# Splitting two projections by columns and keeping weight blocks, so that the norms behind them can start early

## The chip, the cores and the metric

The kernel runs on the 8 cores of one Trainium2 chip, as one program launched once. Cores 0 and 1 take sequence 0 of the batch, cores 2 and 3 sequence 1, and so on; each core produces 1024 of the 2048 tokens of its sequence and reads all weights itself. The metric is device time in microseconds (us) of the slowest core. A program on eight cores has a second, slower state in some executions, in which the cores of one die get a lower TensorE clock; such runs are set aside, and only fast runs are compared.

Words used below: PE is TensorE, the matmul engine; PEld are its weight loads; DVE is VectorE, ACT ScalarE, POOL the engine whose queue issues the weight loads from HBM, SP another issuing queue. PSUM is the memory that matmuls write; the kernel uses it in banks of 512 fp32 columns.

## The reference, cut to what matters

```python
x += concat(y_c, y_m) @ W_out                          # output projection
x += W_down( silu(g) * u ),  [g, u] = dwconv3_causal(RMSNorm(x) @ W_up) + b
x += sigmoid(RMSNorm(x) @ W_pg) * (p[i] @ W_pp)        # gate stage
out = RMSNorm_final(x)

def rmsnorm(x, g):
    y = xf * lax.rsqrt(jnp.mean(xf * xf, axis=-1, keepdims=True) + EPS)
    return (y * g.astype(jnp.float32)).astype(x.dtype)
```

D_MODEL is 2048 (16 blocks of 128 features), D_FF is 5632 (44 blocks), D_PLE 256. The norm runs over features. The kernel keeps features on the 128 partitions and tokens along the columns, so the sum of squares over features needs all 16 blocks of the projection before it, and then a sum over partitions, which PE does as a matmul with a matrix of ones. That is why a norm between two projections tends to stop PE: the next projection's first matmul needs the scaled input, and the scaling needs the last output of the projection before.

## The kernel before

Weights come in blocks of 1024 KB (bf16 in SBUF), into four slots, in the order of tasks. A task is a block and what is done with it; `again` uses a block that is still in its slot.

```python
wo_at = [task(blk(w_out_b, b), 16, 256, wout_task(b, (0, 1), 0)) for b in range(8)]   # pass one: slices 0 and 1
call(norm2_begin)
for n, b in enumerate((4, 5, 6, 7)):                                                   # pass two: slice 2
    again(wo_at[b], wout_task(b, (2,), 8))
    if n == 0:
        call(lambda: [norm2_stat(0), norm2_stat(1)])
    call(lambda n=n: norm2_apply(n // 2, range(8 * (n % 2), 8 * (n % 2) + 8)))
for b in range(4):
    task(blk(w_out_b, b), 16, 256, wout_task(b, (2,), 8))                              # four blocks loaded again
```

So the output projection was already split: 1026 columns in three slices, two in pass one and the third in pass two, with the second norm's sum (`norm2_stat`) and scaling (`norm2_apply`) of the first two under pass two. The down projection and the third norm were not split. The feed-forward part runs in three groups of 16, 16 and 12 blocks of D_FF; each ends in eight down-projection tasks:

```python
def wdown_task(g0, gn, cb, last):
    def consume(slot, Rs):
        if last and cb == 0:
            table_preload()
        for j in range(2):
            f = 2 * cb + j
            ps, Rb = feat_major_proj(slot, Rs, j, aT, RaT[0:gn], gn, wd_slices, k_outer=(cb == 0 and j == 0))
            P.op("dve", ... xres[:, f, 5:1029] += ps ...)          # 1024 columns
            if last:
                sumsq_hook(f, 5, 1024, f == 0)                     # ACT square, DVE add into acc
...
def norm3():
    ...
    norm_finish_sliced(5, own_slices, C_G3, hT, RhT3, Rrs2_3)      # per half: sum on PE, rstd on ACT, 16 scalings on DVE
    P.op("pool", ... ppw <- w_pp ...); P.op("pool", ... pTb <- pT ...)
call(norm3)
```

The gate stage has 32 groups: for half s of the columns and feature block f, 16 matmuls of the gate, 2 of the projection of p, then sigmoid (ACT), product and add (DVE), square (ACT), add into the final norm's sum (DVE). Three pairs of PSUM banks go round. Between the halves stands the final norm's sum of half 0:

```python
for b in range(8):
    pg_task(b, 0)
call(lambda: final_rs(0))                                          # sum on PE, rstd on ACT
for b in range(8):
    pg_task(b, 1)
    call(lambda b=b: final_ops(0, [2 * b, 2 * b + 1]))             # final scaling and store of half 0
call(table_preload)
call(lambda: final_rs(1))
call(lambda: final_ops(1, range(16)))
```

Each engine runs its instructions in program order; waits are on semaphores, placed from what each operation reads and writes.

## Time and profile before

| | before |
|---|---|
| median of 5 runs, slowest core | 1776.13 us (1774.19 to 1777.12) |
| profiled execution | 1774.19 us; spans of the cores 1767.4 to 1772.6 us |
| mean granted TensorE clock of the cores | 0.983 to 0.986 |

How the views are read. A timeline line has the start, the length, the engine, the source line and operation, what it writes and reads, how many instructions are merged, and in brackets how long the engine was idle before it and what ended that idle time. The waits view has, per pair, the total, the count and the longest wait. The table by stretches has the stretch and, by engine, busy time and count, then the granted clock, the DMA share and GB/s. The prediction shows the lines on which it rests. One view that it names but does not show is the list of PE's waits from 540 us on:

```profile
PE psC L1085 <- DVE regE L1080: 7.1, 2, 3.6
...
PE psC L462 <- DVE regE L457: 4.0, 1, 4.0
...
PE psA L1063 <- DVE hT L466: 2.2, 6, 0.7
...
PE psB L869 <- DMA wsl<-w_out_b: 1.7, 1, 1.7
```

L1085 is the final norm's sum (twice, half 0 and half 1), L462 the third norm's sum, L1063 a gate matmul that waits for its scaled input, and L869 the output projection that waits for a reloaded block. These four are what the change works on (of L1085 only half 0's wait).

### The profile page before, as it was taken

To read this page: it belongs to the slowest core of one execution; us is meant where nothing else is said; L and a number is where in the kernel's file an instruction comes from. 1 tells how busy PE (TensorE), PEld (TensorE's weight loads), DVE (VectorE), ACT (ScalarE), POOL (GpSimd) and SP (SyncE) were. 2 spreads that over 40 slices of the span, in tenths; PEclk is the share of its full clock that TensorE was granted. 3 is DMA by queue.
4 is the path that set the end of the run, shared out by engine and by line. 5 is a ranking of instruction groups with operands and counts; after the bars stand their busy time and mean duration, and the time that the engine had idled before them with its cause. 6 is when DMAs were issued, how large, how long until landed. Compare 5 with 4: busy or idle time off the path is not lost.

```text
span 1772.6 us, 27638 instructions; the slowest of 8 cores (1767.4 to 1772.6 us)
## 1 busy us (share of the span) xinstructions
PE 1666.2 (94%) x11268; PEld 1070.4 (60%) x11310; DVE 737.0 (42%) x1092; ACT 389.5 (22%) x567; POOL 69.5 (4%) x134
## 2 busy tenths in 40 slices
PE   1999999989988998999999999999999999998995
PEld 1888868756655665666654466666445666443442
DVE  3543201233354474444431144444212544447556
ACT  3230032322332222222210022222001222222332
POOL 0000000000000000000000000000000000000000
PEclk9999999999999999999999999999999999998997
DMA  9944433433427657344433444333344333346774
GB/s 255 236 103 73 72 55 67 72 54 66 72 49 197 137 89 127 73 80 81 78 72 71 75 81 82 74 72 72 73 83 83 72 72 60 72 84 113 137 147 162
DMA packets 26156, 167.98 MB, mean 95 GB/s; under 512 B 3120, under 2 KB 3120, under 8 KB 8880
## 3 DMA queue, kind: packets, MB, share of 16 engines
q0 software_dynamic: 18976, 131.67, 41.6%
q1 hardware_dynamic: 7056, 34.55, 6.0%
q8 instruction: 91, 1.49, 0.3%
q14 instruction: 33, 0.27, 0.1%
HBM read 289.48 MB, written 8.39 MB: 168 GB/s over the span
## 4 chain that ended last, share of the span: by engine, by line
PE 89%; DVE 4%; DMA 2%; ACT 2%; issue 2%; DVEq 0%; SPq 0%; ACTq 0%; POOLq 0%
PE psB L518 34%; PE psA L518 26%; PE psB L504 9%; PE psA L1063 4%; PE psA L504 4%; PE psB L869 3%; PE psA L869 3%; PE psB L1063 2%; DMA arena<-xsl 2%; DMA wsl<-w_out_b 1%; DVE arena L1092 1%; PE psB L1067 0%; PE psC L413 0%; DVE hT L466 0%; ACT regE L662 0%
## 5 line engine op out<-in xcount | busy, mean ns | idle before, releaser
L518 PE MATMUL psB<-hT,wsl 128*128 128x344 bf16 (+2 forms) x3312 | 501.1, 312 | 8.7 <-DVE yT L739 8.7
L518 PEld LDWEIGHTS psB<-hT,wsl 128*128 128x128 bf16 x3312 | 324.4, 98 | 172.6 <-issue 9.5
L518 PE MATMUL psA<-hT,wsl 128*128 128x344 bf16 (+1 forms) x2160 | 326.8, 311 | 2.0 <-DVE regE L951 2.0
L518 PEld LDWEIGHTS psA<-hT,wsl 128*128 128x128 bf16 x2160 | 211.8, 98 | 109.9 <-issue 2.3
L518 PE MATMUL psA<-yT,wsl 128*128 128x512 bf16 x684 | 154.6, 378 | 2.1 <-DVE yT L988 1.0
L518 PE MATMUL psB<-yT,wsl 128*128 128x512 bf16 x694 | 155.3, 378 | 0.5
L947 ACT ACTIVATE regE<-psA,cst_sb 128x1026 f32<-128x1026 f32 x44 | 53.1, 1207 | 394.2 <-PE psA L518 385.7
L504 PE MATMUL psB<-wsl,hT 128*128 128x256 bf16 x1152 | 128.8, 274 | 0.0
L949 DVE SCALAR_TENSOR_TENSOR regE<-psA,cst_sb,regE 128x1026 f32<-128x1026 f32 x44 | 56.6, 1286 | 165.0 <-ACT regE L947 165.0
L504 PEld LDWEIGHTS psB<-wsl,hT 128*128 128x128 bf16 x1152 | 112.8, 98 | 13.6
L949 DVE SCALAR_TENSOR_TENSOR regE<-psB,cst_sb,regE 128x1026 f32<-128x1026 f32 x44 | 56.6, 1285 | 154.7 <-ACT regE L947 154.7
L518 PEld LDWEIGHTS psA<-yT,wsl 128*128 128x128 bf16 x704 | 68.1, 97 | 84.8 <-issue 1.5
L518 PEld LDWEIGHTS psB<-yT,wsl 128*128 128x128 bf16 x704 | 68.1, 97 | 83.9
L947 ACT ACTIVATE regE<-psB,cst_sb 128x1026 f32<-128x1026 f32 x44 | 53.0, 1205 | 166.8 <-PE psB L518 166.8
L1063 PE MATMUL psA<-hT,wsl 128*128 128x512 bf16 x344 | 85.6, 394 | 3.0 <-DVE hT L466 2.2
L975 ACT ACTIVATE regE<-regE 128x1026 f32<-128x1026 f32 x44 | 46.6, 1058 | 123.5 <-DVE regE L951 123.5
L1006 DVE TENSOR_TENSOR arena<-psB,arena 128x1024 f32<-128x1024 f32 x24 | 29.4, 1225 | 104.4 <-PE psB L518 104.4
L1006 DVE TENSOR_TENSOR arena<-psA,arena 128x1024 f32<-128x1024 f32 x24 | 29.4, 1225 | 93.2 <-PE psA L518 93.2
L1063 PEld LDWEIGHTS psA<-hT,wsl 128*128 128x128 bf16 x352 | 35.2, 100 | 52.0 <-issue 14.3
L869 PE MATMUL psB<-yT,wsl 128*128 128x342 bf16 (+2 forms) x384 | 57.5, 309 | 1.7 <-DMA wsl<-w_out_b 1.7
L951 DVE SCALAR_TENSOR_TENSOR regE<-psA,cst_sb,regE 128x1026 f32<-128x1026 f32 x44 | 56.6, 1286 | 4.6
L951 DVE SCALAR_TENSOR_TENSOR regE<-psB,cst_sb,regE 128x1026 f32<-128x1026 f32 x44 | 56.5, 1285 | 4.6
(161 smaller groups left out, 1371.6 us busy)
## 6 DMA issues: line engine op xcount, KB each, us to landing
wsl<-w_up_b POOLq DMA_DIRECT2D x44, 1024.0 KB, 8.8
wsl<-w_in_b POOLq DMA_DIRECT2D x30, 1024.0 KB, 10.2
wsl<-w_down_b POOLq DMA_DIRECT2D x16, 1024.0 KB, 8.7
wsl<-w_pg_b POOLq DMA_DIRECT2D x16, 1024.0 KB, 8.8
wsl<-w_out_b POOLq DMA_DIRECT2D x12, 1024.0 KB, 12.4
arena<-xr SPq DMA_DIRECT2D x4, 2058.0 KB, 24.5
arena<-xsl SPq DMA_DIRECT2D x8, 1024.0 KB, 11.2
arena<-xsl SPq DMA_DIRECT2D x4, 2048.0 KB, 16.1
```

The lines of the kernel that those rows point to most:

```text
L504: P.op("pe", lambda e, k=k, t=t, ps=ps: e.matmul(ps[:, 0:ncol], lhsT=src[:, k, t * 128:(t + 1) * 128], rhs=slot[:, k, 0:ncol], start=(k == ...
L518: P.op("pe", lambda e, k=k, si=si, c0=c0, w=w: e.matmul(ps[:, si, 0:w], lhsT=slot[:, k, j * 128:(j + 1) * 128], rhs=src[:, k, c0:c0 + w], ...
L869: P.op("pe", lambda e, k=k, ps=ps, c0=c0, w=w, j=j: e.matmul(ps[:, 0:w], lhsT=slot[:, k, j * 128:(j + 1) * 128], rhs=yT[:, k, c0:c0 + w], ...
L947: P.op("act", lambda e: e.activation(out=dst[:, :, :], in_=ps[:, :, 2:344], func=AF.Identity, bias=cs(C_FCB + cidx), scale=w2), reads=Rb + ...
L949: P.op("dve", lambda e: e.scalar_tensor_tensor(out=dst[:, :, :], in0=ps[:, :, 1:343], scalar=w1, in1=dst[:, :, :], op0=ALU.mult, op1=ALU.add),
L951: P.op("dve", lambda e: e.scalar_tensor_tensor(out=dst[:, :, :], in0=ps[:, :, 0:342], scalar=w0, in1=dst[:, :, :], op0=ALU.mult, op1=ALU.add),
L975: P.op("act", lambda e, j=j: e.activation(out=upg[j][:, :, :], in_=upg[j][:, :, :], func=AF.Silu), reads=[Rupg[j]], writes=[Rupg[j]])
L1006: P.op("dve", lambda e, ps=ps, f=f: e.tensor_tensor(out=xres[:, f, 5:1029].rearrange("p (s n) -> p s n", s=2), in0=ps[:, 0:2, 0:512], in1= ...
L1063: P.op("pe", lambda e, k=k, pg_=pg_, j=j: e.matmul(pg_[:, 0:512], lhsT=slot[:, k, j * 128:(j + 1) * 128], rhs=hT[:, k, 512 * s:512 * (s + ...
L1092: P.op("dve", lambda e, k=k, xs=xs: e.scalar_tensor_tensor(out=xs, in0=xs, scalar=cs(C_GF + k), in1=rs2[:, 512 * s:512 * (s + 1)], op0=ALU ...
```

## The change

Its intent: let every norm's sum and scaling of one part of the columns run under the projection of the other part, and avoid the waits for reloaded weight blocks. It has three parts.

1. Output projection: blocks 0 and 1 are loaded a second time, into free memory, while pass one runs; pass two takes them from there, in turn with the blocks still in slots, and reloads only blocks 2 and 3.
2. Last third of the down projection: two passes of 512 columns. Half 0's sum (`norm3_stat(0)`) and scaling run under pass two, half 1's sum comes after the first 16 gate matmuls, and its scaling goes in pairs into gate groups 1 to 8. Blocks 0 to 3 are loaded again (768 KB each). The loads of w_pp and p come earlier, into other memory.
3. The final sum of half 0 moves behind the gate matmuls of the second group of half 1.

```diff
-    wo_at = [task(blk(w_out_b, b), 16, 256, wout_task(b, (0, 1), 0)) for b in range(8)]
+    def load_wo_e():
+        for i in range(2):
+            P.alias(Rwo_e[i], conv_res + mlstm_small_res)
+            P.op("pool", lambda e, i=i: e.dma_start(out=wo_e[i], in_=blk(w_out_b, i)), writes=[Rwo_e[i]], dma=True)
+
+    wo_at = []
+    for b in range(8):
+        wo_at.append(task(blk(w_out_b, b), 16, 256, wout_task(b, (0, 1), 0)))
+        if b == 4:
+            call(load_wo_e)
     call(norm2_begin)
-    for n, b in enumerate((4, 5, 6, 7)):
-        again(wo_at[b], wout_task(b, (2,), 8))
+    second = [("again", 4), ("kept", 0), ("again", 5), ("kept", 1), ("again", 6), ("again", 7), ("load", 2), ("load", 3)]
+    for n, (how, b) in enumerate(second):
+        if how == "again":
+            again(wo_at[b], wout_task(b, (2,), 8))
+        elif how == "kept":
+            call(lambda b=b: wout_task(b, (2,), 8)(wo_e[b], Rwo_e[b]))
+        else:
+            task(blk(w_out_b, b), 16, 256, wout_task(b, (2,), 8))
 ... (cut: norm2_stat and norm2_apply as before; memory of ppw and pTb moved) ...
+    def last_down(cb, s, gn, first_f):
+        def consume(slot, Rs):
+            if s == 0 and cb == 0:
+                table_preload()
+            kcut = gn - 2 if (s == 0 and cb == 0) else gn
+            ... (cut: one PSUM bank for each of two row blocks) ...
+            if kcut < gn:
+                mm(0, range(kcut))
+                mm(1, range(kcut))
+            for j in range(2):
+                f = 2 * cb + j
+                ps, Rb = outs[j]
+                mm(j, range(kcut if kcut < gn else 0, gn))
+                xs = xres[:, f, 5 + 512 * s:5 + 512 * (s + 1)]
+                P.op("dve", ... xs += ps ...)
+                sumsq_late(f == first_f, xs, Rx2[f][s], acc[:, 512 * s:512 * (s + 1)], Racc2[s])
+        return consume
 ... (cut: sumsq_late, norm3_stat, norm3_apply, ple_loads, aliases) ...
+        for cb in range(8):
+            ld_at.append(task(blk(w_down_b, cb, 44)[:, g0:g0 + gn, :], gn, 256, last_down(cb, 0, gn, 0)))
+            if cb == 4:
+                call(ple_loads)
+        for n, cb in enumerate((4, 5, 6, 7)):
+            again(ld_at[cb], last_down(cb, 1, gn, 8))
+            if n == 0:
+                call(lambda: norm3_stat(0))
+            call(lambda n=n: norm3_apply(0, range(3 * n, 3 * n + 3)))
+        for cb in range(4):
+            task(blk(w_down_b, cb, 44)[:, g0:g0 + gn, :], gn, 256, last_down(cb, 1, gn, 8))
+            call(lambda cb=cb: norm3_apply(0, range(12 + 2 * cb, 14 + 2 * cb) if cb < 2 else ()))
 ... in pg_task, between the gate matmuls and the two matmuls of p ...
+                if s == 0 and f == 0:
+                    norm3_stat(1)
+                if s == 1 and f == 1:
+                    final_rs(0)
+                if s == 0 and 1 <= f <= 8:
+                    norm3_apply(1, range(2 * f - 2, 2 * f))
 ...
     for b in range(8):
         pg_task(b, 0)
-    call(lambda: final_rs(0))
     for b in range(8):
         pg_task(b, 1)
```

## The prediction

> **What bounds the kernel now.** I read the page first, then the busy time by stretches around the ends of the phases, then the timeline there, the landing times of single loads, and last the waits of PE.
>
> ```profile
> PE 1666.2 (94%) x11268; PEld 1070.4 (60%) x11310; DVE 737.0 (42%) x1092; ACT 389.5 (22%) x567; POOL 69.5 (4%) x134
> PEclk9999999999999999999999999999999999998997
> PE 89%; DVE 4%; DMA 2%; ACT 2%; issue 2%; DVEq 0%; SPq 0%; ACTq 0%; POOLq 0%
> ```
>
> These are the page's busy line, its clock line and its chain. PE is 94% busy and carries 89% of the chain, so time can only come off where PE stands still or runs slowly, and the change takes no matrix work away. The clock is at 9 (90% or more) everywhere but in two of the last slices. So I look for the places where PE waits within the changed stretch: the output projection (near 560 to 675 us) and everything from the last third of the down projection (1519 us) to the end.
>
> ```profile
> 1520.00:1600.00 80.00, 78.57 (x360) 35.16 (x366) 38.28 (x32) 17.17 (x18) 4.22 (x8) 1.00 0.47 85
> 1600.00:1610.00 10.00, 5.16 (x19) 1.72 (x18) 3.68 (x3) 2.62 (x4) 1.97 (x3) 0.90 0.46 85
> 1610.00:1625.00 15.00, 12.32 (x25) 3.28 (x27) 14.31 (x22) 3.69 (x5) 0.00 (x0) 0.61 0.84 141
> 1625.00:1690.00 65.00, 61.16 (x270) 27.23 (x274) 38.88 (x58) 20.69 (x34) 4.25 (x8) 0.97 0.72 130
> ```
>
> Columns: the stretch, its length, busy us and count of PE, PEld, DVE, ACT, POOL, then granted clock, DMA share, GB/s. Between 1600 and 1625 us PE does 44 matmuls in 25 us. The stretch before does 360 in 80. In 1610 to 1625 us DVE is the full one (14.31 of 15) and the clock falls to 0.61. This is the third norm. The timeline gives its edges:
>
> ```profile
> 1598.01 5.06 PEld L518 LDWEIGHTS psB<-yT,wsl 128*128 128x128 bf16 x24
> ...
> 1607.55 0.30 PEld L462 LDWEIGHTS psC<-regE,cst_sb 128*128 128x128 f32 x2 [4.48 <-issue]
> ...
> 1610.69 21.29 DVE L466 SCALAR_TENSOR_TENSOR hT<-arena,cst_sb,regE 128x512 bf16<-128x512 f32 x32 [3.26 <-ACT regE L393]
> ...
> 1622.76 4.78 PE L1063 MATMUL psA<-hT,wsl 128*128 128x512 bf16 x16
> ...
> 1627.16 0.31 PEld L1067 LDWEIGHTS psB<-yT 128*128 128x128 bf16 x2
> ```
>
> The last down-projection weight load ends at 1598.01 + 5.06 = 1603.07. The sum of squares (a matmul with ones) starts 4.48 us later, after the last add, square and add on DVE and ACT. The gate matmuls then follow the scaling of hT one k at a time, one per 0.665 us (21.29 / 32), until about 1622. The next group still runs slowly. Two groups of 18 matmuls are done at 1627.47.
>
> ```profile
> 1681.55 0.31 PEld L1067 LDWEIGHTS psA<-yT 128*128 128x128 bf16 x2
> ...
> 1685.90 0.30 PEld L1085 LDWEIGHTS psC<-regE,cst_sb 128*128 128x128 f32 x2 [4.04 <-issue]
> ...
> 1691.80 0.31 PEld L1067 LDWEIGHTS psB<-yT 128*128 128x128 bf16 x2
> ```
>
> This is the middle of the gate stage: the final norm's sum for half 0 stands between half 0 and half 1, waits 4.04 us, and the next group of 18 is done only at 1692.11.
>
> ```profile
> 669.23 4.49 PEld L869 LDWEIGHTS psB<-yT,wsl 128*128 128x128 bf16 x32 [2.07 <-issue]
> 669.26 4.81 PE L869 MATMUL psB<-yT,wsl 128*128 128x341 bf16 x32 [1.75 <-DMA wsl<-w_out_b]
> ...
> 675.24 2.18 PEld L968 LDWEIGHTS psA<-hT,wsl 128*128 128x128 bf16 x16 [1.52 <-issue]
> ```
>
> This is the second pass of the output projection. The last reloaded block is late, and then the first up-projection block. I asked for the landing of those two loads alone, issued at 653.83 and 658.48:
>
> ```profile
> wsl<-w_out_b POOLq DMA_DIRECT2D x1, 1024.0 KB, 15.2
> wsl<-w_up_b POOLq DMA_DIRECT2D x1, 1024.0 KB, 16.5
> ```
>
> They land at 669.0 and 675.0, which is when PE goes on. The wait at 675.24 is named by DVE in the waits, but the landing time says it is the load.
>
> **What the Trainium skill says.** "TensorE: Matmul & The Clock Gate", section "What's actually happening": after an idle window of some 3.4 us PE runs at half clock until it has been busy as long. The trace agrees: after the 4.48 us gap and the thin feeding the next gate matmuls come 0.43 us apart, against 3.34 / 15.5 = 0.216 us later, and also after the 4.04 us gap. "DMA: Bandwidth & Descriptors", section "Anatomy of one DMA — SWDGE (gpsimd) path": about 2.0 us fixed plus a part by size. Here a 1024 KB block takes 8.8 us alone (the page's median), while queued blocks land 6.4 to 6.5 us apart, so about 2.3 us is fixed; the skill's rate is not reached, and I use 6.5. "ScalarE: Activation LUTs", section "What ACT_TABLE_LOAD costs": about 1283 ns of load and as much again of drain. The trace has the load at 1.28 us; I see no such drain. "VectorE: DVE Perf Modes", section "The perf-mode tier table": a tensor_tensor on fp32 has only the plain mode. Here 1024 columns take 1.23 us and 512 take 0.69, so time follows width and about 0.15 us is paid per instruction; halves cost a little more DVE.
>
> **The change part by part.**
>
> Part one, the output projection. Its first pass begins at 558.5 and the second at about 633.2 (two thirds into 48 weight loads from 628.54). Eight tasks of 32 matmuls at 6.98 / 48 = 0.1454 us make 37.2 us, and the two sums of squares cost 1.06 us (637.82 to 638.88), so with no wait PE would reach the up projection at 671.5. It gets there at 675.24. The change keeps blocks 0 and 1 in a spare buffer, loaded in the first pass when DMA idles (its share in 600 to 640 us is 0.15), and reloads two blocks, not four. By the same pace blocks 2 and 3 are issued at 638.7 and 649.2 and wanted at 662 and 667; the first up block is issued at 658.5 into an empty queue, lands by 669.5 even with the 10.9 us that a load took here, and is wanted at 671.5. All waits go: 675.24 - 671.5 = 3.7 us. The later stall at 690 to 692 us, where both bank groups wait for their first evacuation, stays.
>
> Part two, the third norm. The last third of the down projection is done in two passes of 512 columns: the same 384 matmuls at 0.216 us, 83 us, plus four reloads of 768 KB (6.5 us to land, one per 5.2 us task, each wanted 15 us after issue: hidden). Sum, rstd and scaling of half 0 lie under pass two: per task of 5.18 us DVE has two evacuations (0.79 with its gap), two adds (0.70) and three scalings (0.665), 5.0 us, just enough. Half 1's sum comes after the first 16 gate matmuls (3.45 us), its last evacuation, square and add needing 0.6 + 0.69 + 0.15 + 0.6 + 0.1 + 0.69 + 0.12 = 2.95 us; no wait. A 512-column sum costs PE about 0.9 us (0.62 measured for 341 columns, by width). Two groups then end at 2 x 3.88 + 0.9 = 8.7 us after the down projection, against 1627.47 - 1603.07 = 24.4 now: 15.7 us saved. At the start of the last third PE waits for the last aT chunk as before; with 21 instead of 22 matmuls placed ahead it loses 0.2 us more.
>
> Part three, half 0's final sum moves behind the second group's gate matmuls of half 1. From 1681.86 to 1692.11 are 10.25 us; one group and the sum need 3.88 + 0.9 = 4.8: 5.5 us saved. The earlier loads of w_pp and p save nothing: they landed at 1614.5 and 1618.2, before PE's need at 1621.9.
>
> What is given back: DVE and ACT lag behind PE in the gate stage. One group's chain repeats every 3.07 us at best (product to product, 1652.46 to 1655.53). With two scalings it is 3.07 + 1.33 = 4.4 against PE's 3.88, so over groups 1 to 8 it falls back 8 x 0.5, on top of some 2.5 us from the switch of tables, to about 6 us behind. Three bank pairs allow the product some 11 us, so PE does not stop; groups 9 to 15 win it back at 0.8 each. The moved final sum, with two table loads, puts ACT and DVE some 3.8 us behind again at group 17. There the budget is thin: two groups with two final scalings need 7.38 of 7.76 us, so 7 pairs win back 0.38 x 7 = 2.7, and about 1 us is left when PE ends. It lengthens the tail (now 1750.4 to 1772.6) by 1.0.
>
> Sum: 3.7 - 0.2 + 15.7 + 5.5 - 1.0 = 23.7 us. 1776.1 - 23.7 = 1752.4.
>
> **The rivals.** First, a DVE bound: if scalings and evacuations cost more than I count, banks come free late and PE waits in pass two or in gate groups 5 to 9. For it: 5.0 of 5.18 and 4.4 against 3.88. Against it: the bank slack of 8 to 11 us. It would give back 2 to 8 us, to 1755 to 1760. Second, DMA: 3 MB of down blocks, 2 MB of output blocks and the earlier w_pp come on top on all eight cores; a late block costs what it is late. For it: queued blocks already land at 6.5 us each. Against it: each is wanted 9 us or more after its expected landing, except the first up block with 2 us. It would leave 1 to 3 us. Third, more gain: without the two waits before it, the stall at 690 us may not lower the clock; 48 matmuls there took 8.86 against 7.03 us, so 1.8 us more. Fourth, the gap moves: if PE met half 1's sum before it is ready, a wait of 1 us and no cold clock.
>
> **Range and chances.** The parts on PE are differences of measured times, certain to perhaps 3 us together; the lag at the end is 0 to 3 us; the rivals weigh more on the slow side. I say 1752, with 1747 to 1760. Faster by over 2% would need 35.5 us, while all the PE waits that I found in these stretches sum to 25: 0.02. Slower by over 2% would need a new bound: 0.01. Within 2%: 0.97.
>
> **What would show it.** Right: no DMA wait at the second pass; no PE gap over 2 us between the end of the down projection and the end of the gate stage; gate groups at 3.88 us from the first; clock near 1.00 there; two short sums on PE; PE's end to span's end 22 to 24 us. Wrong: waits of PE on DVE or ACT in the gate groups, a scaling still running when half 1 begins, a wait on a down block in pass two, or a tail over 25 us.

## The result, and the profile after

| | before | changed |
|---|---|---|
| median | 1776.35 us of 13 runs | 1754.78 us of 7 runs |
| range of the fast runs | 1774.01 to 1777.83 | 1754.27 to 1755.65 |
| ratio, changed over before | | 0.988, 95% interval 0.9869 to 0.989 |

Each has one run in the slow state (2061.2 and 1908.35 us), which is in the median and not in the range or the ratio. The ratio here and below is the mean time of one kernel's fast runs over that of the other's of the same rounds, so it is not quite the ratio of the medians. The kernel is 21.6 us faster by the medians, 1.2%, within the 2% that count as the same.

The page of the changed kernel (busy line, clock line, chain):

```profile
PE 1661.2 (95%) x11310; PEld 1071.5 (61%) x11310; DVE 737.6 (42%) x1123; ACT 391.0 (22%) x583; POOL 71.6 (4%) x138
PEclk9999999999999999999999999999999999999997
PE 89%; DVE 5%; ACT 2%; issue 2%; DMA 2%; DVEq 0%; ACTq 0%; SPq 0%
```

The 8 of the clock line is gone; the last digit, where PE has done its last work, is 7 before and after. The table by stretches, cut at the same events as in the prediction (last third of the down projection, first two gate groups, groups 16 and 17, tail):

```profile
1518.00:1603.00 85.00, 83.71 (x387) 37.40 (x386) 52.44 (x79) 23.37 (x36) 7.80 (x14) 1.00 0.74 126
1603.00:1612.00 9.00, 9.00 (x42) 4.05 (x40) 2.68 (x4) 3.74 (x5) 0.53 (x1) 1.00 1.02 164
...
1666.00:1675.00 9.00, 9.00 (x42) 4.04 (x41) 3.50 (x6) 2.68 (x5) 1.06 (x2) 1.00 0.71 130
...
1729.00:1752.00 23.00, 2.56 (x5) 0.52 (x3) 14.71 (x23) 4.46 (x7) 0.00 (x0) 0.59 0.61 210
```

The first two gate groups now take 9 us at a clock of 1.00 where they took 24.5, and PE is busy in all of it. In the last third DVE works 52 us of 85 where it worked 39.5 of 84 (lines of before in the prediction show 38.28 of 80). PE's waits from 1600 us to the end are down to one, the final sum of half 1:

```profile
PE psC L1172 <- DVE regE L1167: 4.2, 1, 4.2
```

The timeline of the second pass of the output projection (L869) into the up projection (L985, L518):

```profile
666.84 6.93 PEld L869 LDWEIGHTS psB<-yT,wsl 128*128 128x128 bf16 x48
...
673.82 2.30 PEld L985 LDWEIGHTS psA<-hT,wsl 128*128 128x128 bf16 x16
...
691.02 8.53 PEld L518 LDWEIGHTS psA<-hT,wsl 128*128 128x128 bf16 x48 [2.43 <-issue]
691.05 8.86 PE L518 MATMUL psA<-hT,wsl 128*128 128x344 bf16 x48 [2.10 <-DVE regE L968]
```

No line waits for a load any more: the up projection follows 0.05 us after the output projection's last weight load. The stall before 691.02 is still there, and the 48 matmuls after it take 8.86 us where the next 48 take 7.19. (The pause is 2.43 us in the weight loads and 2.10 in PE's matmuls, which lag behind them. The 2.24 us in some of the expectations is neither of the two.) The same block in the kernel before, on core 6 and on core 1:

```profile
692.21 8.86 PE L518 MATMUL psA<-hT,wsl 128*128 128x344 bf16 x48 [1.99 <-DVE regE L951]
```

```profile
693.98 7.19 PE L518 MATMUL psA<-hT,wsl 128*128 128x344 bf16 x48 [1.99 <-DVE regE L951]
```

The stall is equal on both; only on core 6 is the block behind it slow.

The timeline from pass one of the last third (L1046) into the gate stage (L1144 gate, L1154 the two matmuls of p, L1089 the sums of squares):

```profile
1565.99 0.40 PEld L1089 LDWEIGHTS psC<-regE,cst_sb 128*128 128x128 f32 x2
...
1597.92 5.06 PEld L1046 LDWEIGHTS psA<-yT,wsl 128*128 128x128 bf16 x24
...
1603.10 3.33 PEld L1144 LDWEIGHTS psA<-hT,wsl 128*128 128x128 bf16 x16
...
1606.56 0.41 PEld L1089 LDWEIGHTS psC<-regE,cst_sb 128*128 128x128 f32 x2
...
1611.30 0.31 PEld L1154 LDWEIGHTS psB<-regE,yT 128*128 128x128 bf16 x2
```

Half 0's sum stands inside pass two, half 1's after 16 gate matmuls, and two groups end at 1611.61, 8.63 us after 1602.98. And the tail (L1172 final sum, L1179 final scaling):

```profile
1728.71 0.31 PEld L1154 LDWEIGHTS psB<-regE,yT 128*128 128x128 bf16 x2
...
1733.68 0.50 PEld L1172 LDWEIGHTS psC<-regE,cst_sb 128*128 128x128 f32 x2 [4.66 <-issue]
1733.71 2.05 PE L1172 MATMUL psC<-regE,cst_sb 128*128 128x512 f32 x2 [4.19 <-DVE regE L1167]
...
1737.27 10.69 DVE L1179 SCALAR_TENSOR_TENSOR arena<-arena,cst_sb,regE 128x512 f32<-128x512 f32 x16 [2.39 <-ACT regE L393]
```

One core's profile is not enough here, since the slowest core was core 6 before and core 7 after. So I took the start or end of the weight loads that bound each phase on every core and made a table of phase lengths, the median of the eight cores (all in us). The spread over the cores is under 0.1 where none is given.

| phase | before | changed | difference | predicted |
|---|---|---|---|---|
| start to output projection | 558.3 (556.3 to 560.6) | 557.9 (554.7 to 560.7) | -0.4 | 0 |
| output projection, pass one | 74.70 | 74.70 | 0 | 0 |
| output projection, pass two | 41.75 (41.0 to 44.0) | 38.38 | -3.4 | -3.7 |
| up projection to last third of down | 842.28 (842.2 to 844.0) | 844.16 | +1.9 | 0 |
| last third of down projection | 83.93 | 85.00 | +1.1 | +0.2 |
| gate groups 0 and 1 | 24.3 (24.0 to 24.4) | 8.63 | -15.7 | -15.7 |
| gate groups 2 to 15 | 54.39 | 54.39 | 0 | 0 |
| gate groups 16 and 17 | 14.13 (14.0 to 14.1) | 8.63 | -5.5 | -5.5 |
| gate groups 18 to 31 | 54.39 | 54.39 | 0 | 0 |
| tail, from PE's last projection matmul | 22.3 (21.6 to 23.1) | 23.0 (22.5 to 23.7) | +0.7 | +1.0 |
| sum | | | -21.3 | -23.7 |

(Groups 16 and 17 stand for the third part: its new place puts the sum into group 17, so the two are taken together. In the prediction the same difference is 10.25 - 4.8.)

The sum, -21.3 (-0.4 of it ahead of the changed code), fits the -21.6 of the timed runs. Two rows are off: the up projection and the last third.

The row of the up projection is the strange one, since the change does not touch that code. On three cores before it took 843.8 to 844.0 us and on five 842.2 to 842.3; after it takes 844.2 on all eight. The clock records in the trace files, core by core (`prof` prints only their means), show what differs. After the stall in the first up-projection block (PE idle for 1.99 us before, 2.10 after) the clock goes to 0.50 for 3.41 us on all eight cores of the changed kernel, 18.1 to 18.5 us after the up projection's start; before it did so there on two cores, 3 and 6 (core 0, the third with 843.8, had its half clock at the wait for the first block just ahead). All clock changes of a core, from the first to the last, lie on one grid of 3.413 us, and every stretch at half clock is a whole number of such steps (but for the last, which ends with the record). The skill's page "TensorE: Matmul & The Clock Gate", section "What's actually happening", has this as a free-running activity window of 4096 cycles or 3413 ns; the step of these records agrees.

### The profile page after: what moved, and what is told of

Read it like the earlier page. It is cut to its first block, busy times and chain, and to the rows that moved or that the text cites. A ratio compares the mean times of both kernels' runs of the same rounds, so it can differ in the third digit from the quotient of the medians.

```text
span 1752.3 us, 27809 instructions; the slowest of 8 cores (1745.9 to 1752.3 us)
## 1 busy us (share of the span) xinstructions
PE 1661.2 (95%) x11310; PEld 1071.5 (61%) x11310; DVE 737.6 (42%) x1123; ACT 391.0 (22%) x583; POOL 71.6 (4%) x138
## 4 chain that ended last, share of the span: by engine, by line
PE 89%; DVE 5%; ACT 2%; issue 2%; DMA 2%; DVEq 0%; ACTq 0%; SPq 0%
PE psB L518 32%; PE psA L518 25%; PE psB L504 9%; PE psA L504 4%; PE psA L869 3%; PE psB L869 3%; PE psA L1144 3%; PE psA L1046 2%; PE psB L1046 2%; DMA arena<-xsl 2%; PE psB L1144 1%; DVE arena L1179 1%; PE psC L413 1%; ACT regE L662 0%; DVE arena L1160 0%
## 5 line engine op out<-in xcount | busy, mean ns | idle before, releaser
L518 PE MATMUL psB<-hT,wsl 128*128 128x344 bf16 (+2 forms) x3312 | 501.1, 312 | 8.7 <-DVE yT L739 8.7
L518 PEld LDWEIGHTS psB<-hT,wsl 128*128 128x128 bf16 x3312 | 324.5, 98 | 172.6 <-issue 9.5
L518 PE MATMUL psA<-hT,wsl 128*128 128x344 bf16 (+1 forms) x2160 | 327.7, 312 | 2.1 <-DVE regE L968 2.1
L518 PEld LDWEIGHTS psA<-hT,wsl 128*128 128x128 bf16 x2160 | 212.2, 98 | 110.6 <-issue 3.3
L518 PE MATMUL psA<-yT,wsl 128*128 128x512 bf16 x512 | 113.2, 378 | 0.0
L518 PE MATMUL psB<-yT,wsl 128*128 128x512 bf16 x512 | 113.1, 378 | 0.0
L518 PEld LDWEIGHTS psB<-yT,wsl 128*128 128x128 bf16 x512 | 49.5, 97 | 61.0
L518 PEld LDWEIGHTS psA<-yT,wsl 128*128 128x128 bf16 x512 | 49.6, 97 | 60.7
L1144 PE MATMUL psA<-hT,wsl 128*128 128x512 bf16 x352 | 79.6, 379 | 0.0
L1144 PEld LDWEIGHTS psA<-hT,wsl 128*128 128x128 bf16 x352 | 34.4, 98 | 41.5
L1023 DVE TENSOR_TENSOR arena<-psB,arena 128x1024 f32<-128x1024 f32 x16 | 19.6, 1225 | 90.9 <-PE psB L518 90.9
L618 DVE TENSOR_TENSOR arena<-regE,cst_sb 128x256 bf16<-128x256 f32 x36 | 15.3, 425 | 100.5 <-ACT regE L617 100.5
L869 PE MATMUL psA<-yT,wsl 128*128 128x343 bf16 (+2 forms) x368 | 55.0, 309 | 0.0
## 6 DMA issues: line engine op xcount, KB each, us to landing
arena<-xr SPq DMA_DIRECT2D x4, 2058.0 KB, 23.3
```

What stands on the lines that cost most here:

```text
L518: P.op("pe", lambda e, k=k, si=si, c0=c0, w=w: e.matmul(ps[:, si, 0:w], lhsT=slot[:, k, j * 128:(j + 1) * 128], rhs=src[:, k, c0:c0 + w], ...
L869: P.op("pe", lambda e, k=k, ps=ps, c0=c0, w=w, j=j: e.matmul(ps[:, 0:w], lhsT=slot[:, k, j * 128:(j + 1) * 128], rhs=yT[:, k, c0:c0 + w], ...
L1023: P.op("dve", lambda e, ps=ps, f=f: e.tensor_tensor(out=xres[:, f, 5:1029].rearrange("p (s n) -> p s n", s=2), in0=ps[:, 0:2, 0:512], in1= ...
L1144: P.op("pe", lambda e, k=k, pg_=pg_, j=j: e.matmul(pg_[:, 0:512], lhsT=slot[:, k, j * 128:(j + 1) * 128], rhs=hT[:, k, 512 * s:512 * (s + ...
```

## The experiments

The theory before the experiments: the three parts act independently, each by taking PE's waits away; the up projection loses 1.9 us because PE's stall there now always falls into one window of the clock's grid, while before the varying load waits moved it about; the rest of the shortfall is half 0's sum, which costs PE 0.9 us within pass two and which the prediction left out. The rivals are named in each expectation. Where a diff says nothing else, it is against the changed kernel. All results were correct against the reference. Runs e1 to e4 were on one chip, e5 to e8 on a second, e9 to e11 on a third, each with its own runs of the kernel before.

Phase lengths, medians of eight cores, for all runs (us). A range is given where cores differ, except for the tail, which differs by 1 to 2 us over the cores of every run, so that its medians tell little under 1 us:

| run | pass two of output | up projection | last third | groups 0, 1 | groups 16, 17 | tail |
|---|---|---|---|---|---|---|
| before | 41.75 | 842.28 | 83.93 | 24.3 | 14.13 | 22.3 |
| changed | 38.38 | 844.16 | 85.00 | 8.63 | 8.63 | 23.0 |
| e1 | 38.38 | 844.15 | 83.93 | 24.41 | 14.13 | 22.6 |
| e2 | 41.99 (40.5 to 42.8) | 842.2 on 3 cores, 843.9 on 5 | 85.00 | 8.63 | 8.63 | 22.2 |
| e3 | 38.38 | 844.15 | 85.00 | 8.63 | 12.44 | 22.4 |
| e4 | 38.38 | 844.15 | 84.14 | 20.45 | 8.63 | 23.3 |
| e5 | 39.62 | 842.4 on 6 cores, 844.1 on 2 | 85.00 | 8.63 | 8.63 | 23.1 |
| e6 | 40.82 | 842.42 | 85.00 | 8.63 | 8.63 | 22.9 |
| e7 | 38.38 | 841.07 | 85.00 | 8.63 | 8.63 | 23.1 |
| e8 | 38.38 | 844.15 | 83.55 | 8.63 | 8.63 | 21.8 |
| e9 | 38.38 | 844.15 | 85.00 | 8.63 | 8.63 | 23.2 |
| e10 | 38.38 | 844.15 | 85.00 | 8.63 | 8.63 | 22.3 |
| e11 | 38.38 | 841.07 | 83.55 | 8.63 | 8.63 | 21.7 |

### e1: the output projection's part alone

Against the kernel before:

```diff
+    def load_wo_e(): ...                                  # and the order 4, kept 0, 5, kept 1, 6, 7, load 2, load 3
-            P.alias(r, conv_res + mlstm_small_res)
+            P.alias(r, conv_res + mlstm_small_res + Rwo_e)
```

> The output projection's change alone (spare copies of two weight blocks, two reloads instead of four), all else as before. Theory (waits go, but the stall behind them then always costs a half-clock window): second pass to up projection 38.4 us on every core against a median of 41.75 before, a half-clock window of 3.4 us in the first up-projection stretch on all eight cores, so that stretch is 844.2 against 842.3; in all about 1.5 us faster than before, near 1774.8. Rival (the prediction's third rival: fewer waits, so the clock stays up): no half-clock window there, 842.3, in all 3 to 5 us faster. Second rival (the new loads collide): the second pass is longer than 38.4.

Measured: fast runs 1773.72 to 1775.15 us, before 1774.79 to 1779.74; ratio 0.9982 (0.9969 to 0.9995). Pass two takes 38.38 us and the up projection 844.15 on every core, and the clock records have the half-clock window behind the stall on all eight. So the phases did as the theory said, and the rival that had the clock stay up is wrong, as is the second, that the new loads collide. The time by the ratio is 3.2 us better, more than the 1.5 of the theory, but the interval (0.9 to 5.5 us) holds that too; it would also hold the first rival's 3 to 5 us. The runs of before scatter over 5 us on this chip. A reason that fits, but is only argued: the metric is the slowest core, and before the slowest core is one that had long load waits or a half-clock window, so making all cores alike gains more than the median shows.

### e2: parts two and three alone

```diff
-    second = [("again", 4), ("kept", 0), ...]             # all of part one undone
+    for n, b in enumerate((4, 5, 6, 7)): again(...)       # as in the kernel before
```

> The third norm's and the final sum's change alone, the output projection as before. If the parts add up: pass two and gate stage as in the changed kernel (85.0, 8.6, 8.6 us), second pass of the output projection 41 to 44 us with waits on loads as before, the half-clock window in the up projection on some cores only; in all 19 to 20.5 us faster than before, near 1756.3. Rival (the earlier parts help the later ones, or their loads do): less than 18 us faster.

Measured: 1757.93 to 1758.79 us, ratio 0.9891 (0.9877 to 0.9905), 19.4 us faster by that ratio. The phases of parts two and three are those of the changed kernel to 0.01 us, and pass two varies with the load waits again. The half clock in the up projection is there on three cores (2, 5, 7); on two more (0 and 4) it came at the load wait just ahead. The parts add up, and the loads of one do not disturb the others.

### e3: the final sum of half 0 back between the halves

```diff
-                if s == 1 and f == 1:
-                    final_rs(0)
...
     for b in range(8):
         pg_task(b, 0)
+    call(lambda: final_rs(0))
```

> The changed kernel, but half 0's final sum back between the two halves of the gate stage. Theory: PE waits some 4 us there and runs at half clock after it, groups 16 and 17 take about 14.1 us instead of 8.6; the lag at the end is a little smaller, so the tail is 22.3 instead of 23.0; 4.8 to 5.5 us slower than the changed kernel, near 1760. Rival (the wait was hidden behind the lag of DVE that the scalings make): more than 5.5 us slower, since DVE comes later to its last add than before. Rival two: the move only shifts the loss to the tail, under 2 us slower.

Measured: fast runs 1756.06, 1757.64 and 1759.48 us, ratio 0.9888 (0.9868 to 0.9907). Groups 16 and 17 take 12.44 us: 3.8 us more than in the changed kernel, where 5.5 were expected. The timeline (L1170 is the final sum):

```profile
1671.39 0.30 PEld L1170 LDWEIGHTS psC<-regE,cst_sb 128*128 128x128 f32 x2 [4.04 <-issue]
...
1672.36 3.12 PEld L1144 LDWEIGHTS psA<-hT,wsl 128*128 128x128 bf16 x15 [0.33 <-issue]
```

The wait is the old 4.04 us, but the gate matmuls after it run at full pace, 15 weight loads in 3.12 us; no core has a half-clock window there. A gap of 4.04 us in the weight loads is longer than a window of the grid and yet cost nothing in clock: by the clock records it lay across an edge on every core, and of PE's 3.58 us of idle time no window held more than 1.98. So of part three's 5.5 us about 3.8 are the wait and 1.7 the half clock, and the second share depends on how the stage lies to the grid. The tail is 0.5 us shorter, of 0.7 expected. In all 3.3 us by the phases; the ratio gives 1.4 us. The ratio alone does not exclude rival two (under 2 us); the phases do, since the tail gives back only 0.5 us. The first rival, a longer wait than before, is wrong: it is 4.04 us again.

### e4: split, but nothing hidden

```diff
         for n, cb in enumerate((4, 5, 6, 7)):
             again(ld_at[cb], last_down(cb, 1, gn, 8))
-            if n == 0:
-                call(lambda: norm3_stat(0))
-            call(lambda n=n: norm3_apply(0, range(3 * n, 3 * n + 3)))
...
+            if cb == 3:      # after pass two: sum and 16 scalings of half 0, then of half 1
+                call(lambda: [f_() for si in range(2) for f_ in (lambda si=si: norm3_stat(si), lambda si=si: norm3_apply(si, range(16)))])
```

(and `norm3_stat(1)`, `norm3_apply(1, ...)` taken out of the gate groups)

> The changed kernel with the down projection still in two passes with its four reloads, but both halves' sums and all scalings after pass two, as before. It tells the price of splitting from the worth of hiding. Theory: pass one and two 84.1 us (0.2 over before, no load waited for), then the first two gate groups take about 23 us (24.3 before less some 1.5, since the last evacuation, square and add are 512 wide); in all 14 us slower than the changed kernel, near 1769. Rival (the reloads or the narrower evacuations cost PE time): the passes take over 85 us. Rival two (splitting itself gains): under 10 us slower than the changed kernel.

Measured: 1764.33 to 1766.45 us, ratio 0.9932 (0.9918 to 0.9946). The last third takes 84.14 us, as the theory has it, so the rival that the reloads or the narrower evacuations cost PE time is wrong: the 0.2 us over before is the longer wait for the last aT chunk at the start (weight loads pause 1.75 us on every core, before 1.51). But the first two gate groups take 20.45 us, not 23. The timeline says why:

```profile
1604.19 0.40 PEld L1089 LDWEIGHTS psC<-regE,cst_sb 128*128 128x128 f32 x2
...
1607.17 0.30 PEld L1089 LDWEIGHTS psC<-regE,cst_sb 128*128 128x128 f32 x2 [2.58 <-issue]
1607.45 21.29 DVE L1095 SCALAR_TENSOR_TENSOR hT<-arena,cst_sb,regE 128x512 bf16<-128x512 f32 x32 [0.51 <-ACT regE L393]
```

Half 0's sum starts as soon as PE is free, since its inputs are long there, and the scaling starts 3.3 us after it (1607.45 against 1604.19). In the kernel before, the scaling starts at 1610.69, 7.6 us after the last weight load. The theory had moved both sums by the narrower evacuation alone and overlooked this. So splitting alone, at the price of 0.2 us, saves 24.3 - 20.45 = 3.9 us of the 15.7; hiding the sums and the scaling saves the other 11.8 (20.45 - 8.63), of which 0.86 is given back in the last third (see below). Rival two's mark, under 10 us slower than the changed kernel, is met by the ratio (0.0052 x 1776 = 9.2 us); by the phases it is 11.8 - 0.9 + 0.3 = 11.2. That 84.14 becomes 85.00 in the changed kernel is half 0's sum inside pass two, 0.86 us.

### e5 and e6: the same stall, shifted against the clock's grid

```diff
+    def filler(n):
+        for _ in range(n):
+            P.op("pe", lambda e: e.matmul(psC[:, 0:256], lhsT=ones_bf, rhs=cbf[:, 0:256], start=True, stop=True),
+                 reads=[Rcbf], writes=[RpsC])
+    call(lambda: filler(11))        # e5; 22 in e6; ahead of the up projection
```

> The changed kernel with 11 needless matmuls of 256 columns (about 1.2 us of PE at full clock) between the output projection and the up projection; outputs are right. In all eight traces of the changed kernel a 3.4 us half-clock window follows the 2.24 us stall of PE in the first up-projection block, and all clock changes of a core lie on one grid of 3.413 us. Theory (what counts is how much of the stall falls in one window of the grid): shifted by 1.2 us the stall still lies within the same window, so the half-clock window stays on all eight cores and the kernel is about 1.2 us slower than the changed one. Rival (the length of the gap decides): the same here; the next run tells them apart.

> The same with 22 needless matmuls (about 2.4 us). Theory: the 2.24 us stall now lies across an edge of the grid, about half in each window, no half-clock window follows on most or all cores, and the stretch behind is 1.7 to 1.9 us shorter; in all only 0.5 to 0.7 us slower than the changed kernel though PE does 2.4 us more, and not slower than the run with 11. Rival (the length of the gap decides): the half-clock window stays on all eight cores and the kernel is 2.4 us slower than the changed one.

Measured, e6: 1756.93 to 1759.3 us, ratio 0.9872 (0.9855 to 0.989). Only two runs of e5 were fast (1756.43 and 1758.15 us), too few for a ratio. The first up-projection block after the stall, in the timelines of e5 on core 3, of e5 on core 0 and of e6:

```profile
690.88 8.77 PE L518 MATMUL psA<-hT,wsl 128*128 128x344 bf16 x48 [2.15 <-DVE regE L974]
```

```profile
687.66 7.19 PE L518 MATMUL psA<-hT,wsl 128*128 128x344 bf16 x48 [2.10 <-DVE regE L974]
```

```profile
696.67 7.19 PE L518 MATMUL psA<-hT,wsl 128*128 128x344 bf16 x48 [2.10 <-DVE regE L974]
```

The stall is nearly the same in all three, 2.10 to 2.15 us; the half clock follows it in the first only. With 22 needless matmuls no core has the half-clock window and the up projection takes 842.42 us on all eight: 2.44 us of useless work are paid by 1.73 saved. The length of the gap does not decide, and that rival is wrong. For e5 my expectation failed in part: the window stayed on cores 3 and 6 alone, not on all eight. The clock records say why. The stall ends 17.1 to 17.2 us after the up projection's start, and a window's edge lies at 17.1 on these two and between 16.8 and 17.0 on the six others, so the shift of 1.24 us had put the edge on the very end of the stall, closer than I had reckoned. Two or three tenths of the stall outside the window were enough to keep the clock.

How much idle time in a window is needed can be read from the records of before, e2 and e3 taken together. An idle time of PE of 1.99 us that lay wholly within a window halved the clock each time (the stall; before, cores 3 and 6; e2, cores 2, 5 and 7), and so did 1.96 (a load wait; e2, core 0), while waits of 1.95 and 1.86 us wholly within one did not (before, core 1; e2, core 7). Of a longer gap that an edge cuts, parts of up to 1.98 us did not (e3). So for one unbroken gap the limit lies near 2.0 us of 3.41; the ends of matmuls are modelled in these records, so it can't be had more exactly. Broken up by single matmuls, a little less was enough (1.83 to 1.94 us in e4, at the norm's sums).

Why before and after differ, then: on all sixteen cores of the two profiles the output projection starts 5.0 to 5.4 us after the clock's last return to full speed, that is, at the same place of the grid. Without load waits, the work from there to the stall is the same on each core, so the stall lies at the same place of the grid on each, and it happens to be a bad one. Before, the load waits (2.6 to 5.6 us by core) spread it. Why the start of the output projection keeps to the grid on all cores was not tried. The traces show a part of it: some 228 us into the span the same weight load lies 1.8 us into a window on cores 0, 1, 4 and 7 of before and 3.0 to 3.3 us on the other four; the first four alone then have a half-clock window near 245 us, and at 248 us all eight lie within 0.5 us of one another. In the changed kernel cores 6 and 7 are drawn to the others in the same way. So a half-clock window can itself pull the cores together on the grid; whether that is the whole reason stays open.

### e7: first gate block evacuated in two steps

```diff
-    def conv_evac(ps, Rb, dst, Rdst, cidx):
+    def conv_evac(ps, Rb, dst, Rdst, cidx, lo=0, hi=3):
+        Rb = Rb[lo:hi]
... (slices lo to hi in its three operations) ...
                 for sis in ((0, 1), (2,)):
                     ... (matmuls of both row blocks for these slices) ...
+                    if sis == (0, 1):
+                        conv_evac(*early[0], upg[0], Rupg[0], 0, 0, 2)
...
-                conv_evac(ps, Rb, upg[j], Rupg[j], c)
+                conv_evac(ps, Rb, upg[j], Rupg[j], c, 2 if jj == 0 and j == 0 else 0, 3)
```

> The changed kernel with the first gate block of the up projection evacuated in two steps (slices 0 and 1 before slice 2's matmuls are done), so that its banks come free before PE wants them. Theory: no stall of 2.24 us there and no half-clock window behind it: the stretch from the up projection's start to the last third of the down projection falls from 844.2 to 840.2 us, in all about 3.9 us faster than the changed kernel. Rival (the stall is due to the late third slice of hT, not to the banks): the stall stays and the time is the same within 0.5 us.

Measured: fast runs 1751.62, 1755.05, 1756.49 and 1777.67 us (in the last one die is 0.7% longer and its lowest core at a clock of 0.973), ratio 0.9884 (0.9802 to 0.9967): the timing is inconclusive. The up projection takes 841.07 us on all eight cores, 3.1 us less than in the changed kernel, of 3.9 expected. The timeline:

```profile
692.20 6.98 PEld L518 LDWEIGHTS psA<-hT,wsl 128*128 128x128 bf16 x48
...
700.20 6.86 PEld L518 LDWEIGHTS psB<-hT,wsl 128*128 128x128 bf16 x48 [1.02 <-issue]
```

The stall before the first L518 block is gone and no core has a half-clock window. A new gap of 1.02 us in the weight loads (0.70 us of PE) stands one block later, where the other bank group is wanted: the wait was moved on by one block and made shorter, which is about the 0.8 us that is missing. The rival (the late third slice of hT) is wrong.

### e8: thirty matmuls ahead

```diff
-            outs = []
-            for j in range(2): ...
+            todo = [(0, s), (1, s)]
+            if cb == 0:
+                todo = [(0, 0), (1, 0), (0, 1)] if s == 0 else [(1, 1)]
... (the loops over j go over todo; half 1's sum then starts with f == 0) ...
```

> The changed kernel with half 1 of the first row block moved up to pass one of the last third, so that 30 matmuls instead of 20 lie before the first that needs the last chunk of the gated product. Theory: the 1.8 us wait at the start of pass one is gone, both passes together take 83.3 us instead of 85.0 (82.9 of matmuls and 0.9 of a sum less what overlaps), in all 1.7 us faster than the changed kernel. Rival (the wait moves to a load or a bank in the next blocks): less than 0.5 us faster.

Measured: fast runs 1753.41, 1755.5 and 1778.15 us (again one with a lowest clock of 0.973), ratio 0.9896 (0.9799 to 0.9994), too wide to tell. By the phases the last third takes 83.55 us, 1.45 less than 85.00, of 1.7 expected, on all cores. The timeline shows the first 36 weight loads (L1049 is the down projection's matmul here) without a break, where the changed kernel stops for 1.76 us after 21:

```profile
1520.90 7.59 PEld L1049 LDWEIGHTS psA<-yT,wsl 128*128 128x128 bf16 x36
```

The tail is 1.1 us shorter as well, which nobody expected. The tail's final sum takes 1.1 to 1.45 us here over the eight cores where it takes 2.05 in the changed kernel. The clock records show the cause: the sum starts 4.7 us after PE's last projection matmul in both, but the clock falls 4.0 to 4.3 us after it in the changed kernel and 5.3 to 5.7 us after it here. The shift by 1.45 us moved the wait against the grid. The rest of the 1.1 us is within the scatter of the tail.

### e9, e10 and e11: the changed kernel again, a warm tail, and all three repairs

e9 is the changed kernel without an edit.

> The changed kernel itself, once more, on the chip and in the rounds of the next two, so that they can be set beside it. It should be 1.2% faster than before (ratio 0.988), with the half-clock window in the first up-projection blocks on all eight cores and a final sum that starts 4.2 us after PE's last matmul and runs at half clock.

Measured: 1753.57 to 1755.59 us, ratio 0.9876 (0.9863 to 0.9889); half-clock window on all eight cores. The result repeats on this chip.

e10:

```diff
+    def keep_warm():
+        for _ in range(32):
+            P.op("pe", lambda e: e.matmul(psC[:, 0:256], lhsT=ones_bf, rhs=cbf[:, 0:256], start=True, stop=True),
+                 reads=[Rcbf], writes=[RpsC])
+    call(keep_warm)
     call(table_preload)
     call(lambda: final_rs(1))
```

> The changed kernel with 32 needless matmuls of 256 columns (3.5 us) after the last projection matmul, where PE would else wait 4.2 us for the last add; outputs are right. Theory (the final sum takes 2.05 us instead of 1.02 only because the wait fell into a half-clock window): the sum takes about 1.0 to 1.3 us, the tail from PE's last projection matmul to the end is 0.8 to 1.0 us shorter than the changed kernel's 22.9, all else is the same. Rival (needless matmuls delay the sum): no gain or a loss.

Measured: 1752.01 to 1755.18 us, ratio 0.987 (0.9857 to 0.9883), 1.1 us under e9 by the ratios, within both intervals. The tail is 22.3 us, against 23.2 in e9. The final sum in the timeline:

```profile
1735.18 1.10 PE L1172 MATMUL psC<-regE,cst_sb 128*128 128x512 f32 x2 [0.72 <-DVE regE L1167]
```

It takes 1.10 us instead of 2.05, as expected, and no needless matmul delays it: PE still waits 0.72 us for the last add. On all eight cores the sum takes 1.10 us. The gain in the tail is the expected 0.9, though the tail scatters by more than that over the cores (21.3 to 23.3), so only the sum's own 0.95 us is sure.

e11 has the edits of e7, e8 and e10 together.

> The changed kernel with all three repairs: first gate block evacuated in two steps, thirty matmuls ahead at the start of the last third, and PE kept busy before the final sum. If their gains add up (3.1 + 1.4 + 0.9 us as the phases of the single runs showed or are expected to show), 5.4 us faster than the changed kernel in the same rounds, near 1749.5, and 1.5% faster than before. Rival (a new phase on the clock's grid takes some of it back): a half-clock window appears elsewhere in the up projection or the gate stage and 1.7 us are lost.

Measured: four runs at 1748.5, 1748.55, 1748.59 and 1751.23 us, one at 1762.93 that still counts as fast though one die ran at 0.981 to 0.985 and 0.5% longer than the other, and one slow; ratio with that run 0.9865 (0.9839 to 0.9891). Its interval overlaps e9's, so by the ratios this is not settled; but the four undisturbed runs do not overlap with e9's four (1753.57 to 1755.59), and lie 5.5 us lower in the mean. By the phases 3.1 + 1.45 + 1.5 = 6.0 us are gone, and no half-clock window appears between the output projection and the tail on any core, so the rival is wrong. This version is faster than the kernel before by the ratio; that it is faster than the changed kernel rests on these four runs, picked after the fact, and on the phases.

## Why the prediction was right or wrong, point by point

The predicted time was 1752 us with a range of 1747 to 1760; measured 1754.78. The mechanism of each part was right, and the gain was overestimated by about 2 us in 23.7.

- **Load waits of the output projection** (3.7 us): right. 3.4 on the median core and 3.6 on core 6, whose trace the prediction read; the first up block, issued at 660.71, landed 10.0 us later and was wanted at 673.82.
- **"The later stall at 690 to 692 us ... stays"**: the stall stayed, but its clock cost did not stay the same. This is the step with the largest miss, +1.9 us on the median core. The prediction looked at core 6 alone, one of the two cores on which the half-clock window stood there before; on five others it did not, and after the change all eight have it. On the core that it read, the step holds: core 6 went from 843.9 to 844.2. The third rival saw that the load waits and the half clock are linked, and had the sign wrong: not having waits before the stall is what put it into one window (e1, e5, e6). Its 1.8 us set a length (8.86) against a spacing (7.03); like with like, 8.86 - 7.19, it is 1.7.
- **Third norm, first two gate groups** (15.7 us): right to 0.1. e4 adds what the prediction did not separate: 3.9 of it come from the split, 11.8 from hiding the sums and the scaling.
- **Last third** ("it loses 0.2 us more"): the 0.2 is right (84.14 in e4), but the sum left out half 0's sum on PE inside pass two, 0.86 us (85.00 against 84.14). The prediction counted the sums of half 1 and of part three at 0.9 each and not this one, which it has run "under pass two"; for PE it is not hidden, it is PE's own work.
- **Final sum of half 0** (5.5 us): right; e3 shows that 3.8 of it are the wait and 1.7 a half-clock window that need not have followed.
- **Lag of ACT and DVE** (1.0 us): right in kind, 0.7 measured in the tail; the wait before the final sum grew from 3.57 to 4.19 us, 0.6. The gate groups never waited for a bank, at 3.885 us each from the first to the last.
- **The rivals**: DVE did not become the bound (groups 2 to 31 unchanged to 0.01 us), and no load was late (e1, e4). The gap did not move either: PE does half 1's sum at 1606.56 with no idle time before it. All three were given small weight, rightly. One reading beside them fails without touching the sum: that 2.3 us of a load's time is fixed. Blocks of 768 KB land alone in 6.4 to 6.5 us and blocks of 1024 KB in 8.7 to 8.8, so the time goes almost in proportion to the size.
- **The chances**: "within 2%" had 0.97, and the measured 1.2% is there. The prediction saw that the waits to be had sum to 25 us, under the 35.5 that 2% need.

## What to carry to other kernels

When a norm or another reduction stands between two projections, split the projection ahead of it by columns: the split alone lets the first part's reduction be ready at the end, and hiding the element-wise part behind the other pass gains most; the price is reloading some weights, which cost PE nothing here, where each load was issued well ahead. Count every small matmul that is put "under" other work on PE as PE's own time. And when waits are removed ahead of a stall that stays, look at the clock on every core, not on one: the stall's price depends on where it lies in the clock's window, and the cure is to remove the stall, as e7 did, not to shift it.

## What the Trainium skill lacked or had wrong

- "TensorE: Matmul & The Clock Gate", section "What's actually happening": it gives at least one idle window of about 3.4 us as the condition for half clock. Here about 2.0 us without matmuls within one window of 3.413 us were enough (1.99 us halved the clock, 1.95 and 1.86 did not), and a longer idle time of 3.58 us across an edge did not halve it (e3). The grid of the windows itself is as the page says: every change of every core lies on it.
- No page that I read says that removing waits can line the cores up, so that a stall costs the half-clock window on all of them: 2 of 8 cores before, 8 of 8 after.
- "ScalarE: Activation LUTs", section "What ACT_TABLE_LOAD costs": about 1.38 us of drain is given on top of the load's 1.283. In the gate stage of the changed kernel the load starts 0.01 us after the activation before it ends (1609.22) and the next activation starts 1.30 us later (1610.52), so only the load's 1.28 us shows.
- "DMA: Bandwidth & Descriptors", section "Anatomy of one DMA — SWDGE (gpsimd) path": its fit, 2.0 us plus bytes at 436e3 per us, would give 4.4 us for the 1024 KB that the load of a block writes and 6.8 us for the 2048 KB of fp32 that it reads (estimates from that page, which does not say which of the two counts when a load converts). With all eight cores loading, these loads take 8.8 us alone and, when queued, land 6.4 to 6.5 us apart. A fixed part of 2 us does not show either: a block of 768 KB takes 6.4 to 6.5 us alone, 2.3 us less for 256 KB less.
